# Layer 1's weight folds, its q swaps and the place of its folded projection in a two-layer encoder

## The chip, the cores and the metric

The kernel runs on one core of one Trainium2 chip. Every time is in device microseconds of that core; one launch does the whole computation. A profile is one execution taken by the hardware profiler.

## What is computed

Two layers over 272 tokens (16 learned tokens and 256 of the input) of width 2048, in float32. Cut to what matters here:

```
h = RMSNorm(x)
q, k, v, f, ga, gf = split(h @ W_in)                # 8 q heads, 2 kv heads of 128; f has 8 groups of 128 channels
q, k = rope_2d(RMSNorm(q)), rope_2d(RMSNorm(k))     # rotary: swaps neighbouring 32-channel quarters of a head
a = softmax(q k^T / sqrt(128)) v @ W_attn_br
s = Re(2-D DFT of f over positions and group channels) @ W_four
x = x + (sigmoid(ga) * a + sigmoid(gf) * s) @ W_out
x = x + (silu(dwconv3(RMSNorm(x) @ W_up_gate)) * (RMSNorm(x) @ W_up_val)) @ W_down
```

## The kernel before

Activations lie with channels on the 128 partitions and tokens along the row. Every float32 matrix product is made of three matmuls: each operand is split into a rounded high part and a rest (`wh` and `wl` for weights, `xHL` for activations), and high x high, high x rest and rest x high are summed.

**The weight stream.** All weights of both layers come in chunks of 512 KB ([128, 4, 256]), in one list `order` that is written out ahead (from L140). `load_raw` (L176 to L180) issues a chunk's load on SyncE (SP, line L179) into one of four `raw` buffers. `split_w` makes `wh` on ScalarE (ACT, L213) and `wl` on VectorE (DVE, L214); there are three buffers of each. `advance` keeps loads up to four chunks ahead of the splits and splits two ahead of the matmuls. `group` (from L242) runs one pair of output tiles: four chunks for an input of 2048 channels, 24 matmuls to a chunk (L270 to L272).

**Shadow work.** Smaller work (statistics, rotary, attention, Fourier steps) is written as generators that `push` puts into a list. `group` calls `step` after every second pair of products, 16 times in a group of four chunks; `step` lets one generator run to its next `yield n`, where n is the number of steps to wait. `until(hold, flag)` forces generators on until a flag is set. The instructions of each engine are then put in an order by the framework's scheduler, so a generator's place in the source is a wish, not the final place.

**The folds.** Layer 1's Fourier branch uses that a cosine is even and a sine odd: sums and differences of paired weight columns (and rows) do half the matmuls. They are made by `prefold` (L427 to L444) during the FFN of layer 0: 32 tiles of 512 KB, each loaded to `pfi` (L433), added and subtracted on VectorE into `pfo` (L439), and stored to `fw` in DRAM (L444). All transfers are issued on SP, among the weight loads. Layer 1 reads `fw` as part of its stream: 16 chunks for the folded projection f4, and two for each of eight `s` groups.

**The start of layer 1.** Groups k and v come first, then q group 0, then f4 (`folded_f`, from L661), then q groups 1, 2 and 3, then gates and branches. f4 uses all eight PSUM banks and runs 18 matmuls in each of its 16 chunks; it calls no `step`. `fold_pair` prepares its folded input on VectorE and ACT, four pairs ahead and four during f4. `folded_chan` then does the channel DFT.

**The q path.** `head_evac` takes a q group out of PSUM (L745 on ACT, L746 on VectorE). `q_stage` (from L848) makes the head sums, swaps the quarters with four DMAs of 68 KB (`swap`, L756 to L760, issued on ACT at L759), and after seven or eight steps does the rotary (`rope`, L762 to L767: L763, L764, L765 and L767 on VectorE, L766 on ACT). The same swap serves k. In layer 1 the q tiles `qH` and `qL` share their memory with f4's result `E` and with the v tile, so `q_stage` of group 0 waits until after the channel DFT of f4.

Of the kernel before, what the change touches and what calls it, by code (L numbers as in the profile page):

```python
# [16 lines left out]
P = 128  # L17
# [111 lines left out]
def encoder_kernel(ctx, tc, xT, params, consts, bmat, cfold, csign, w_fl, w_f64c, w_in, w_abr, w_four, w_f64, w_out, w_up, w_down, outT):  # L129
# [11 lines left out]
    for l in range(DEPTH):  # L141
        def g(w, mg, k0, k1):
            return [(w[l, mg, c], CW) for c in range(k0 // CW, k1 // CW)]
        if l == 0:
            f01 = [g(w_in, IN_F + i, 0, KT) for i in range(2)]
            order.append(((l, "f01"), [ch for pr in zip(*f01) for ch in pr]))
            for i in range(2, 4):
                order.append(((l, "f", i), g(w_in, IN_F + i, 0, KT)))
        order.append(((l, "k", 0), g(w_in, IN_K, 0, KT)))
        order.append(((l, "v", 0), g(w_in, IN_V, 0, KT)))  # L150
        for i in range(4):
            order.append(((l, "q", i), g(w_in, IN_Q + i, 0, KT)))
            if l == 1 and i == 0:
                order.append(((l, "f4"), [(fw[kt], CW) for kt in range(KT)]))
        for half in range(2):
            for kind, j in BRANCH_ORDER[half]:
                w, off, n = {"ga": (w_in, IN_GA, KT), "gf": (w_in, IN_GF, KT), "s": (w_four, 0, 8), "a": (w_abr, 0, 8)}[kind]
                chs = [(fw[KT + 2 * j + c], CW) for c in range(2)] if (l, kind) == (1, "s") else g(w, off + j, 0, n)
                order.append(((l, kind, j), chs))
            for mg in range(8):  # L160
                order.append(((l, "o", half, mg), g(w_out, mg, 8 * half, 8 * half + 8)))
        k0 = 0
        for c, n in enumerate(FF_SPLIT):
            for i in range(k0 // MG, (k0 + n) // MG):
# [55 lines left out]
    def push(gen, wait=0):  # L220
        shadow.append([wait, gen])
# [204 lines left out]

    def prefold(pool):  # L427
        src = [w_fl[k] for k in range(KT)] + [w_four[1, j, c] for j in range(NG) for c in range(2)]
        ins, outs = {}, {}
        for j in range(len(src) + 2):  # L430
            if j < len(src):
                ins[j] = pool.tile([P, CW, MG * P], F32, tag="pfi", name=f"pfi{j}", bufs=2)
                nc.sync.dma_start(ins[j], src[j])  # L433
            yield 2
            if 0 <= j - 1 < len(src):
                a, o = ins.pop(j - 1), pool.tile([P, CW, MG * P], F32, tag="pfo", name=f"pfo{j}", bufs=2)
                half = (lambda t_, q: t_[:, :, q * P:(q + 1) * P]) if j - 1 < KT else (lambda t_, q: t_[:, 2 * q:2 * q + 2])
                for q, op in ((0, ALU.add), (1, ALU.subtract)):
                    nc.vector.tensor_tensor(half(o, q), half(a, 0), half(a, 1), op=op)  # L439
                    yield 1  # L440
                outs[j - 1] = o
            yield 2
            if j >= 2:
                nc.sync.dma_start(fw[j - 2], outs.pop(j - 2))  # L444

    def norm_stats(holder):
        ps = psum.tile([P, 512], F32, tag="aux", name="ps_nst")
# [25 lines left out]
    for l in range(DEPTH):  # L473
# [4 lines left out]
        hold = {}  # L478

        with tc.tile_pool(name=f"mix{l}", bufs=1) as mp:  # L480
            E = mp.tile([P, 4, 2, TH] if last else [P, NG, T], F32, tag="q1", name="E")
            e64 = mp.tile([2 * NG, TH], F32, tag="u", name="e64", bufs=2) if last else None
            AHn = 3 * 4 * T
            ALn = 2 * 4 * T
# [176 lines left out]
            def folded_f(slots, E):  # L661
# [6 lines left out]
                for k in range(KT):  # L668
                    i = st["next"]
                    advance(i + 1 + LOOK)  # L670
                    pump(i)
                    h, lo_ = splits.pop(i)
                    st["next"] += 1
                    sl = slots[k % NS]
                    for g in (0, 1, 2, 3):
                        for e in range(2):
                            w = slice(e * P, (e + 1) * P)
                            o2 = ps[g][e][:, :2 * TH].rearrange("p (r n) -> p r n", r=2)
                            nc.tensor.matmul(o2, h[:, g, w], sl[:, e], start=k == 0, stop=False)
                            if g == e == 0:  # L680
                                for r in range(2):
                                    nc.tensor.matmul(p64, w64s[:, k, :], sl[:, 0, r, :], start=False, stop=False)
                            nc.tensor.matmul(ps[g][e][:, :TH], lo_[:, g, w], sl[:, e, 0, :], start=False, stop=k == KT - 1)
                        pump()
                        if k == KT - 1:
                            for e in range(2):
                                nc.scalar.copy(E[:, g, e, :], ps[g][e][:, TH:2 * TH])
                                nc.vector.tensor_tensor(E[:, g, e, :], ps[g][e][:, :TH], E[:, g, e, :], op=ALU.add)
                            if g == 0:
                                nc.scalar.copy(e64, p64)  # L690
                    if k % 2 and k + NS < KT:
                        fold_pair((k + NS - 1) // 2, slots)
# [63 lines left out]
            def swap(hp):  # L756
                qs = rt("qs")
                for b in range(4):
                    nc.scalar.dma_start(qs[32 * b:32 * b + 32, :, :], hp[32 * (b ^ 1):32 * (b ^ 1) + 32, :, :])  # L759
                return qs  # L760

            def rope(hp, qs, H, L):  # L762
# [51 lines left out]
                until(hold, "keys")  # L814
            else:
                drain()
            vt = mp.tile([P, NKV, 3 * P], F32, tag="q2", name="vt")
            for m in range(MG):
                nc.vector.tensor_tensor(vt[:, m, P:3 * P], ps[m][:, NM:T], rstdB[:, NM:T], op=ALU.mult)
                nc.vector.tensor_tensor(vt[:, m, 0:P].rearrange("p (a b) -> p a b", b=NM), _rep(ps[m][:, 0:NM], P // NM),  # L820
# [26 lines left out]

            def q_stage(i, qp, qsq):  # L848
                kv, j = i // 2, i % 2
                sl = slice(2 * i, 2 * i + 2)  # L850
# [18 lines left out]
                rope(qp, qs, qH[:, sl, :], qL[:, sl, :])  # L869
                if j:  # L870
                    rqs.append(rq)
                    if kv == 0:
# [10 lines left out]
            def attention(kv, rq):  # L883
                nc.vector.tensor_scalar(rq, rq, 1.0 / math.sqrt(HD), None, op0=ALU.mult)
                qm = mp.tile([P, 2, 2, 4, NM], F32R, tag="qm", name="qm")
                for j, src in enumerate((qH, qL)):
                    nc.scalar.copy(qm[:, j], src[:, 4 * kv:4 * kv + 4, 0:NM].bitcast(F32).unsqueeze(1).to_broadcast([P, 2, 4, NM]))
# [7 lines left out]
                def scores(item):  # L895
                    if item is None:
                        lh, ll, rcol = qmh, qml, rq[:, 8:9]
                    else:
                        h, i = item
                        c0, c1 = BLK[1 + i]  # L900
                        lh, ll = qH[:, 4 * kv + h, c0:c1], qL[:, 4 * kv + h, c0:c1]
# [44 lines left out]
                        nc.vector.tensor_tensor(x3, src[32:48, 2], x3.bitcast(F32), op=ALU.subtract)  # L946

                def values(h):
                    hg = 4 * kv + h
# [6 lines left out]
                    nc.scalar.copy(qH[:, hg, lo:T], po[:, :W])  # L956
                    nc.vector.tensor_tensor(qL[:, hg, lo:T], po[:, :W], qH[:, hg, lo:T].bitcast(F32), op=ALU.subtract)
# [20 lines left out]
                while ready:  # L978
                    values(ready.pop(0))
                    yield 1  # L980

            for i in range(4):
                ps = group((l, "q", i), xr(lo), W)
                qq = head_evac(ps, prm[:, P_QN + l:P_QN + l + 1], "qp", lo)
                if last and i == 0:
                    until(hold, "vt")
                    until(hold, "ahead")
                    folded_f(slots, E)
                    o1_tiles()
                    push(folded_chan(E), 1)  # L990
                    q0 = qq
                    continue
                if i == int(last):
                    until(hold, "vt")
                    until(hold, "fold")
                    qH = mp.tile([P, NH, T], F32R, tag="q1", name="qH")
                    qL = mp.tile([P, NH, T], F32R, tag="q2", name="qL")
                    if last:
                        push(q_stage(0, *q0), 1)
                push(q_stage(i, *qq), 4)  # L1000


            def gate(kind, i):
# [11 lines left out]
            for half in range(2):  # L1015
                mH = mL = None
                for kind, i in BRANCH_ORDER[half]:
# [19 lines left out]
                    else:  # L1037
                        if mH is None:
# [5 lines left out]
                        ps = group((l, "a", i), lambda kt: (qH[:, kt, lo:T], qL[:, kt, lo:T]), W)  # L1044
# [140 lines left out]
```

## Time and profile before

| | |
|---|---|
| median of 3 runs | 2612.56 us (2611.66 to 2616.31) |
| the profiled execution's own time | 2610.09 us |
| its span, first to last instruction | 2608.3 us |
| granted TensorE clock, mean | 0.997 |
| PE busy | 2578.4 us, 99% |
| VectorE, ACT busy | 1719.6 us, 1215.6 us |
| moved by DMA | 499.19 MB, mean 191 GB/s |

The stages lie in the span as follows: layer 0's input and mixing up to about 533 us, its FFN to 1355, layer 1's k, v, q and f4 to 1482, its gates, branches and output to 1856, its FFN to the end. A page of the profile gives busy time by engine; its groups and the other views name an instruction by line, engine and the tiles that it writes and reads (`wl<-raw,wh`). "Idle before" is the time for which the engine stood in front of an instruction, and the arrow names what came last of what it waited for. SPq is SyncE's queue, which issues DMAs; PE is TensorE's matmul and PEld its weight load, which overlap, so that a busy PE is not one at full speed. A table by stages gives for each stretch the length, then busy time and count by engine, the clock, the DMA engines' share and GB/s.

### The profile page before, as it was taken

To read this page: it belongs to the slowest core of one execution; us is meant where nothing else is said; L and a number is where in the kernel's file an instruction comes from. 1 tells how busy PE (TensorE), PEld (TensorE's weight loads), DVE (VectorE), ACT (ScalarE), POOL (GpSimd) and SP (SyncE) were. 2 spreads that over 40 slices of the span, in tenths; PEclk is the share of its full clock that TensorE was granted. 3 is DMA by queue.
4 is the path that set the end of the run, shared out by engine and by line. 5 is a ranking of instruction groups with operands and counts; after the bars stand their busy time and mean duration, and the time that the engine had idled before them with its cause. 6 is when DMAs were issued, how large, how long until landed. Compare 5 with 4: busy or idle time off the path is not lost. (4 is left out here: it accounts for less than half of the span.)

```text
span 2608.3 us, 47795 instructions
## 1 busy us (share of the span) xinstructions
PE 2578.4 (99%) x19604; PEld 2507.6 (96%) x19604; DVE 1719.6 (66%) x2742; ACT 1215.6 (47%) x1762; POOL 20.5 (1%) x40
## 2 busy tenths in 40 slices
PE   9999999999899999999999999999999999999999
PEld 8999999999899999999999999999999998899988
DVE  7687767777666445656568777666766665566654
ACT  5455434543344334444445455445555543344543
POOL 0000000000000000000000000000000000000000
PEclk9999999999999999999999999999999999999999
DMA  6545655589865555555556446656555556555564
GB/s 232 167 147 162 194 183 187 181 283 331 300 232 178 172 177 176 173 178 173 175 178 205 142 143 196 192 191 193 186 185 186 185 187 187 186 186 186 186 198 158
DMA packets 142810, 499.19 MB, mean 191 GB/s; under 512 B 16368, under 2 KB 23152, under 8 KB 142592
## 3 DMA queue, kind: packets, MB, share of 16 engines
q1 hardware_dynamic: 136944, 491.23, 58.2%
q10 hardware_dynamic: 5648, 4.92, 0.6%
q8 instruction: 153, 2.51, 0.4%
q14 instruction: 65, 0.53, 0.1%
HBM read 474.43 MB, written 18.87 MB: 189 GB/s over the span
## 5 line engine op out<-in xcount | busy, mean ns | idle before, releaser
L214 DVE TENSOR_TENSOR wl<-raw,wh 128x1024 fp32r<-128x1024 f32 (+1 forms) x850 | 1036.2, 1221 | 717.5 <-ACT wh L213 712.8
L213 ACT CAST wh<-raw 128x1024 fp32r<-128x1024 f32 (+1 forms) x850 | 887.8, 1047 | 1013.9 <-issue 152.8
L272 PE MATMUL ps_ug<-xHL,wl 128*128 128x272 f32 (+1 forms) x1408 | 401.5, 286 | 2.6 <-DVE wl L214 2.5
L270 PE MATMUL ps_ug<-xHL,wh 128*128 128x272 f32 (+1 forms) x1408 | 402.2, 286 | 1.9 <-ACT wh L213 1.9
L271 PE MATMUL ps_ug<-xHL,wh 128*128 128x272 f32 (+1 forms) x1408 | 402.1, 286 | 0.0
L270 PEld LDWEIGHTS ps_ug<-xHL,wh 128*128 128x128 f32 x1408 | 265.4, 189 | 3.8 <-ACT wh L213 2.8
L272 PEld LDWEIGHTS ps_ug<-xHL,wl 128*128 128x128 f32 x1408 | 264.4, 188 | 4.1 <-DVE wl L214 3.9
L271 PEld LDWEIGHTS ps_ug<-xHL,wh 128*128 128x128 f32 x1408 | 265.5, 189 | 0.1
L266 PE MATMUL ps_uv<-xHL,wh 128*128 128x512 f32 x704 | 247.7, 395 | 0.0
L266 PE MATMUL ps_d<-gHL,wh 128*128 128x512 f32 x664 | 233.1, 395 | 0.0
L271 PE MATMUL ps_d<-gHL,wh 128*128 128x272 f32 (+1 forms) x744 | 214.4, 288 | 0.0
L270 PE MATMUL ps_d<-gHL,wh 128*128 128x272 f32 (+1 forms) x744 | 214.1, 288 | 0.0
L272 PE MATMUL ps_d<-gHL,wl 128*128 128x272 f32 (+1 forms) x744 | 214.0, 288 | 0.0
L270 PE MATMUL ps_uv<-xHL,wh 128*128 128x272 f32 x704 | 204.9, 291 | 8.1 <-ACT wh L213 8.1
L272 PE MATMUL ps_uv<-xHL,wl 128*128 128x272 f32 x704 | 203.9, 292 | 2.7 <-DVE wl L214 2.7
L271 PE MATMUL ps_uv<-xHL,wh 128*128 128x272 f32 x704 | 204.6, 291 | 0.0
L267 PE MATMUL ps_uv<-xHL,wl 128*128 128x256 f32 x704 | 197.7, 281 | 0.0
L267 PE MATMUL ps_d<-gHL,wl 128*128 128x256 f32 x664 | 186.6, 281 | 0.0
L266 PEld LDWEIGHTS ps_uv<-xHL,wh 128*128 128x128 f32 x704 | 132.4, 188 | 29.9
L266 PEld LDWEIGHTS ps_d<-gHL,wh 128*128 128x128 f32 x664 | 125.0, 188 | 29.2
L270 PE MATMUL ps_ga<-xHL,wh 128*128 128x272 f32 (+1 forms) x512 | 148.2, 289 | 0.0
L270 PE MATMUL ps_gf<-xHL,wh 128*128 128x272 f32 (+1 forms) x512 | 147.2, 287 | 0.0
(322 smaller groups left out, 5854.0 us busy)
## 6 DMA issues: line engine op xcount, KB each, us to landing
raw<-in_w_up SPq DMA_DIRECT2D x352, 512.0 KB, 3.5
raw<-in_w_in SPq DMA_DIRECT2D x191, 512.0 KB, 3.6
raw<-in_w_down SPq DMA_DIRECT2D x176, 512.0 KB, 3.5
raw<-in_w_out SPq DMA_DIRECT2D x64, 512.0 KB, 3.6
raw<-in_w_abr SPq DMA_DIRECT2D x32, 512.0 KB, 3.6
fw<-pfo SPq DMA_DIRECT2D x32, 512.0 KB, 7.7
raw<-fw SPq DMA_DIRECT2D x32, 512.0 KB, 4.2
raw<-in_w_four SPq DMA_DIRECT2D x16, 512.0 KB, 3.8
```

What stands on the lines that cost most here:

```text
L213: nc.scalar.copy(h[:, a:b], r[:, a:b])
L214: nc.vector.tensor_tensor(lo[:, a:b], r[:, a:b], h[:, a:b].bitcast(F32), op=ALU.subtract)
L266: nc.tensor.matmul(o2, h[:, c, sl], ab, start=kt == 0, stop=False)
L267: nc.tensor.matmul(o, lo[:, c, sl], ab[:, 0, :], start=False, stop=kt == nk - 1)
L270: nc.tensor.matmul(o, h[:, c, sl], a, start=kt == 0, stop=False)
L271: nc.tensor.matmul(o, h[:, c, sl], b, start=False, stop=False)
L272: nc.tensor.matmul(o, lo[:, c, sl], a, start=False, stop=kt == nk - 1)
```

## The change

Four edits, all in the code above.

- `prefold` has one loop step less. It loads tile j and in the same place issues the store of tile j - 1; then waits 12 steps, adds, waits 3, subtracts, waits 3, and waits 12 more. Before, the waits were 2, 1, 1 and 2, the add was for the tile loaded one turn earlier, and the store came at the end of the turn after that.
- `swap` issues its four DMAs on SP.
- In layer 1 the folded projection comes after q group 1, in `order` and in the loop; q_stage of groups 0 and 1 is pushed when the group is done. To make that possible `E` and the v tile of layer 1 have buffers of their own (`q1b`, `q2b`), and the q tiles are two of four heads each instead of one of eight.
- In the last chunk of `folded_f` the output groups run in the order 2, 3, 0, 1.

```diff
-            if l == 1 and i == 0:
+            if l == 1 and i == 1:
                 order.append(((l, "f4"), [(fw[kt], CW) for kt in range(KT)]))
...
-        for j in range(len(src) + 2):
+        outs = {}
+        for j in range(len(src) + 1):
             if j < len(src):
-                ins[j] = pool.tile([P, CW, MG * P], F32, tag="pfi", name=f"pfi{j}", bufs=2)
-                nc.sync.dma_start(ins[j], src[j])
-            yield 2
-            if 0 <= j - 1 < len(src):
-                a, o = ins.pop(j - 1), pool.tile([P, CW, MG * P], F32, tag="pfo", name=f"pfo{j}", bufs=2)
+                a = pool.tile([P, CW, MG * P], F32, tag="pfi", name=f"pfi{j}", bufs=2)
+                nc.sync.dma_start(a, src[j])
+            if j:
+                nc.sync.dma_start(fw[j - 1], outs.pop(j - 1))
+            yield 12
+            if j < len(src):
+                o = pool.tile([P, CW, MG * P], F32, tag="pfo", name=f"pfo{j}", bufs=2)
...
                 for q, op in ((0, ALU.add), (1, ALU.subtract)):
                     nc.vector.tensor_tensor(half(o, q), half(a, 0), half(a, 1), op=op)
-                    yield 1
-                outs[j - 1] = o
-            yield 2
-            if j >= 2:
-                nc.sync.dma_start(fw[j - 2], outs.pop(j - 2))
+                    yield 3
+                outs[j] = o
+            yield 12
...
-                    for g in (0, 1, 2, 3):
+                    for g in ((2, 3, 0, 1) if k == KT - 1 else (0, 1, 2, 3)):
...
                 for b in range(4):
-                    nc.scalar.dma_start(qs[32 * b:32 * b + 32, :, :], hp[32 * (b ^ 1):32 * (b ^ 1) + 32, :, :])
+                    nc.sync.dma_start(qs[32 * b:32 * b + 32, :, :], hp[32 * (b ^ 1):32 * (b ^ 1) + 32, :, :])
...
+            qH, qL = [], []
             for i in range(4):
                 ps = group((l, "q", i), xr(lo), W)
                 qq = head_evac(ps, prm[:, P_QN + l:P_QN + l + 1], "qp", lo)
-                if last and i == 0:
-                    until(hold, "vt")
-                    until(hold, "ahead")
...
+                if last:
+                    if i in (0, 2):
+                        until(hold, "vt" if i == 0 else "fold")
+                        for t_, n in ((qH, "q1"), (qL, "q2")):
+                            t_.append(mp.tile([P, 4, T], F32R, tag=n + "ab"[i // 2], name=n))
...
+                push(q_stage(i, *qq), 4)
+                if last and i == 1:
                     until(hold, "ahead")
                     folded_f(slots, E)
                     o1_tiles()
                     push(folded_chan(E), 1)
```

More of the change, by code (lines that the diff above doesn't have):

```diff
@@ L428, in prefold @@
         src = [w_fl[k] for k in range(KT)] + [w_four[1, j, c] for j in range(NG) for c in range(2)]
-        ins, outs = {}, {}
-        for j in range(len(src) + 2):
+        outs = {}
+        for j in range(len(src) + 1):
             if j < len(src):
-                ins[j] = pool.tile([P, CW, MG * P], F32, tag="pfi", name=f"pfi{j}", bufs=2)
-                nc.sync.dma_start(ins[j], src[j])
-            yield 2
-            if 0 <= j - 1 < len(src):
-                a, o = ins.pop(j - 1), pool.tile([P, CW, MG * P], F32, tag="pfo", name=f"pfo{j}", bufs=2)
-                half = (lambda t_, q: t_[:, :, q * P:(q + 1) * P]) if j - 1 < KT else (lambda t_, q: t_[:, 2 * q:2 * q + 2])
+                a = pool.tile([P, CW, MG * P], F32, tag="pfi", name=f"pfi{j}", bufs=2)
[5 more added lines that the diff above has]
+                o = pool.tile([P, CW, MG * P], F32, tag="pfo", name=f"pfo{j}", bufs=2)
+                half = (lambda t_, q: t_[:, :, q * P:(q + 1) * P]) if j < KT else (lambda t_, q: t_[:, 2 * q:2 * q + 2])
                 for q, op in ((0, ALU.add), (1, ALU.subtract)):
                     nc.vector.tensor_tensor(half(o, q), half(a, 0), half(a, 1), op=op)
-                    yield 1
-                outs[j - 1] = o
-            yield 2
-            if j >= 2:
-                nc.sync.dma_start(fw[j - 2], outs.pop(j - 2))
+                    yield 3
+                outs[j] = o
+            yield 12
     def norm_stats(holder):
@@ L480, in encoder_kernel @@
         with tc.tile_pool(name=f"mix{l}", bufs=1) as mp:
-            E = mp.tile([P, 4, 2, TH] if last else [P, NG, T], F32, tag="q1", name="E")
+            E = mp.tile([P, 4, 2, TH] if last else [P, NG, T], F32, tag="q1b" if last else "q1", name="E")
             e64 = mp.tile([2 * NG, TH], F32, tag="u", name="e64", bufs=2) if last else None
@@ L816, in encoder_kernel @@
                 drain()
-            vt = mp.tile([P, NKV, 3 * P], F32, tag="q2", name="vt")
+            vt = mp.tile([P, NKV, 3 * P], F32, tag="q2b" if last else "q2", name="vt")
             for m in range(MG):
@@ L849, in q_stage @@
                 kv, j = i // 2, i % 2
-                sl = slice(2 * i, 2 * i + 2)
+                sl = slice(2 * j, 2 * j + 2)
                 if j == 0:
@@ L868, in q_stage @@
                 yield 8 - j
-                rope(qp, qs, qH[:, sl, :], qL[:, sl, :])
+                rope(qp, qs, qH[kv][:, sl, :], qL[kv][:, sl, :])
                 if j:
@@ L886, in attention @@
                 for j, src in enumerate((qH, qL)):
-                    nc.scalar.copy(qm[:, j], src[:, 4 * kv:4 * kv + 4, 0:NM].bitcast(F32).unsqueeze(1).to_broadcast([P, 2, 4, NM]))
+                    nc.scalar.copy(qm[:, j], src[kv][:, :, 0:NM].bitcast(F32).unsqueeze(1).to_broadcast([P, 2, 4, NM]))
                 qmh, qml = (qm[:, j].rearrange("p r h t -> p (r h t)") for j in range(2))
@@ L900, in scores @@
                         c0, c1 = BLK[1 + i]
-                        lh, ll = qH[:, 4 * kv + h, c0:c1], qL[:, 4 * kv + h, c0:c1]
+                        lh, ll = qH[kv][:, h, c0:c1], qL[kv][:, h, c0:c1]
                         rcol = rq[:, 2 * h + i:2 * h + i + 1]
@@ L948, in values @@
                 def values(h):
-                    hg = 4 * kv + h
                     po = psum.tile([P, 512], F32, tag="aux", name="ps_pv")
@@ L955, in values @@
                     nc.tensor.matmul(po[:, :W], V3[:, kv, :], PH[:, 2, h, lo:T], start=False, stop=True)
-                    nc.scalar.copy(qH[:, hg, lo:T], po[:, :W])
-                    nc.vector.tensor_tensor(qL[:, hg, lo:T], po[:, :W], qH[:, hg, lo:T].bitcast(F32), op=ALU.subtract)
+                    nc.scalar.copy(qH[kv][:, h, lo:T], po[:, :W])
+                    nc.vector.tensor_tensor(qL[kv][:, h, lo:T], po[:, :W], qH[kv][:, h, lo:T].bitcast(F32), op=ALU.subtract)
                 items = [None] + [(h, i) for h in range(4) for i in range(2)]
@@ L984, in encoder_kernel @@
                 qq = head_evac(ps, prm[:, P_QN + l:P_QN + l + 1], "qp", lo)
-                if last and i == 0:
-                    until(hold, "vt")
+                if last:
[3 more added lines that the diff above has]
+                            t_.append(mp.tile([P, 4, T], F32R, tag=n + "ab"[i // 2], name=n))
+                elif i == 0:
+                    until(hold, "vt")
+                    until(hold, "fold")
+                    for t_, n in ((qH, "q1"), (qL, "q2")):
+                        t = mp.tile([P, NH, T], F32R, tag=n, name=n)
+                        t_ += [t[:, 0:4], t[:, 4:8]]
+                push(q_stage(i, *qq), 4)
+                if last and i == 1:
                     until(hold, "ahead")
@@ L990, in encoder_kernel @@
                     push(folded_chan(E), 1)
-                    q0 = qq
-                    continue
-                if i == int(last):
-                    until(hold, "vt")
[L995 to L1000, printed above, removed]
             def gate(kind, i):
@@ L1043, in encoder_kernel @@
                             mL = mLf[:, :8 * T].rearrange("p (k t) -> p k t", k=8)
-                        ps = group((l, "a", i), lambda kt: (qH[:, kt, lo:T], qL[:, kt, lo:T]), W)
+                        ps = group((l, "a", i), lambda kt: (qH[kt // 4][:, kt % 4, lo:T], qL[kt // 4][:, kt % 4, lo:T]), W)
                         for m in range(MG):
```

## Prediction

> **What bounds the kernel now.** I read the page first, then the table by stages, then the waits of the worst stage, then the transfers. The page:
>
> ```profile
> span 2608.3 us, 47795 instructions
> PE 2578.4 (99%) x19604; PEld 2507.6 (96%) x19604; DVE 1719.6 (66%) x2742; ACT 1215.6 (47%) x1762; POOL 20.5 (1%) x40
> DMA  6545655589865555555556446656555556555564
> ```
>
> TensorE is busy for 99% of the span, so only places where it waits or runs slowly can give anything. The DMA row shows one bump, slices 8 to 10. The table by stages covers it, with an undisturbed stretch below for scale:
>
> ```profile
> 533.00:620.00 87.00, 86.66 (x689) 86.36 (x688) 67.26 (x106) 38.23 (x51) 1.22 (x1) 1.00 0.94 320
> 620.00:727.00 107.00, 91.77 (x662) 87.59 (x661) 71.37 (x107) 38.46 (x50) 0.00 (x0) 0.95 0.90 315
> 740.00:1234.00 494.00, 494.00 (x3936) 494.00 (x3936) 276.44 (x356) 208.34 (x252) 0.00 (x0) 1.00 0.54 175
> ...
> 1394.00:1432.00 38.00, 35.16 (x293) 33.57 (x290) 31.55 (x47) 23.21 (x41) 0.24 (x2) 1.00 0.78 242
> 1432.00:1464.00 32.00, 32.00 (x260) 30.97 (x259) 22.38 (x56) 14.18 (x34) 2.16 (x5) 1.00 0.45 133
> 1464.00:1482.00 18.00, 16.00 (x116) 15.34 (x115) 13.52 (x29) 9.01 (x18) 0.00 (x0) 0.91 0.51 148
> ```
>
> The columns after the length are busy time and count of PE, weight load, DVE, ACT, POOL, then clock, DMA share, GB/s. The long stretch gives the pace: 494.00 / 3936 = 0.1255 us per matmul, so one weight chunk (24 matmuls, one 512 KB load) takes 3.01 us. At that pace 689 matmuls take 86.5 us and 662 take 83.1: the first layer's FFN loses 0.5 + 23.9 = **24.4 us** from 533 to 727. The third row from layer 1 loses 18.00 - 116 x (32.00 / 260) = **3.7 us**, and the folded projection before it (1394 to 1432) has 38.00 - 35.16 = **2.8 us** idle. Those are the three places the change can pay in.
>
> Who is late in the first of them (waits from 533 to 730, then SP's own, then the transfers from 533 to 727):
>
> ```profile
> ACT wh L213 <- DMA raw<-in_w_up: 50.2, 22, 5.0
> PE ps_uv L270 <- ACT wh L213: 8.1, 3, 2.9
> ```
> ```profile
> SPq L433 <- DVE pfo L439: 57.9, 17, 7.0
> ```
> ```profile
> DMA packets 16877, 61.59 MB, mean 317 GB/s; under 512 B 1878, under 2 KB 1878, under 8 KB 16862
> raw<-in_w_up SPq DMA_DIRECT2D x55, 512.0 KB, 6.3
> fw<-pfo SPq DMA_DIRECT2D x32, 512.0 KB, 7.7
> pfi<-in_w_fl SPq DMA_DIRECT2D x16, 512.0 KB, 6.1
> pfi<-in_w_four SPq DMA_DIRECT2D x16, 512.0 KB, 5.2
> ```
>
> The weight split (ACT, L213) waits 50.2 us for loads. The folds of layer 1's weights add 32 loads and 32 stores of the same 512 KB to 55 weight loads, and together they get 317 GB/s at a DMA share of 0.90 to 0.94, against 175 GB/s when the weights go alone. This stretch is bound by the supply of weights, and nothing else in the kernel loses so much.
>
> **The change part by part.**
>
> 1. *The folds.* The fold's four waits in steps sum to 30 instead of 6 per tile, and a group has 16 steps, so the source reads as if a tile came every 7.5 chunks. The built order does not follow that: as the scheduler arranged SP, the first fold load stands behind weight load 173 in both kernels, and the last fold store behind load 226 before and 243 after. The folds are spread over 70 chunks where they had 53, not over 240. So, with 0.524 MB per transfer:
>  - before: (53 + 64) x 0.524 = 61.3 MB, at 317 GB/s 193.5 us; TensorE needs 53 x 3.01 = 159.5. The gap is 34.0, of which 24.4 was lost, so the four weight buffers ahead took up 9.6 (three chunks).
>  - after: (70 + 64) x 0.524 = 70.3 MB, 221.6 us; TensorE needs 70 x 3.01 = 210.8. The gap is 10.8, less the same 9.6: 1.2.
>
>  I take **2 us lost** where 24.4 were, a gain of 22.4. Bounds: nothing lost, a gain of 24.4; or the supply of the stretch's poorest third with no help from the buffers, 70.3 MB at 310 GB/s = 226.6, 15.8 lost, a gain of 8.6:
>
> ```profile
> 533.00:580.00 47.00, 46.66 (x371) 46.37 (x370) 37.58 (x63) 22.97 (x31) 1.22 (x1) 1.00 0.92 310
> ```
>
>  The store of a tile is now issued behind the load of the next, so SP meets results that are mostly done. The work itself is the same 64 halves (0.684 us each, below) on VectorE.
>
>  A part of the 24.4 is not waiting. The time line:
>
> ```profile
> 680.18 0.29 PE L272 MATMUL ps_ug<-xHL,wl 128*128 128x272 f32 x1
> 683.40 0.59 PE L270 MATMUL ps_uv<-xHL,wh 128*128 128x272 f32 x1 [2.94 <-ACT wh L213]
> ...
> 688.90 0.43 PE L271 MATMUL ps_uv<-xHL,wh 128*128 128x272 f32 x1
> ```
>
>  After 2.94 us of idling, matmuls take 0.43 us for 0.29 for over 5 us, and the mean clock of the stage is 0.95: 5% of 107 us, 5.4 us. Idling alone is 107.00 - 91.77 = 15.2. The rest lies in small late starts. [...]
>
> 2. *The swaps, from ACT to SP.* Each swap is four issues:
>
> ```profile
> qs<-qp ACTq DMA_DIRECT2D x32, 68.0 KB, 4.1
> r<-in_w_f SPq DMA_DIRECT2D x16, 64.0 KB, 4.3
> ```
> ```profile
> L759 ACTq DMA_DIRECT2D qs<-qp x4: 592/614/1597, 1468.8 to 1471.8; - x4
> L759 ACTq EVENT_SEMAPHORE  x1: 3792/3792/3792, 1465.0 to 1465.0; - x1
> ```
> ```profile
> 1475.21 0.72 DVE L763 TENSOR_TENSOR qs<-qs,cst 128x544 f32<-128x544 f32 x1 [2.08 <-DMA qs<-qp]
> ```
> ```profile
> 1477.82 0.39 PE L272 MATMUL ps_q<-xHL,wl 128*128 128x258 f32 x1 [1.71 <-DVE wl L214]
> ```
>
>  This is the 3.7 us at 1464: ACT stood 3.79 us at a swap for VectorE's q, the splits behind it waited, the swap left late, VectorE waited 2.08 for it, and TensorE 1.71 for the split after that. 40 issues x 0.61 = 24 us of ACT go; ACT is 47% busy, so they are worth nothing by themselves, but its standing still is. On SP the weight loads queue behind the swap: about 2.4 us of issue each time. They run four buffers ahead (4 x 3.01 = 12 us) and outside the folds land in 3.5, so the cover is over 6 us; without it ten swaps would cost 24. A transfer of this size from SP lands in 4.3 us against 4.1, so the swap is not much later.
>
> ```profile
> raw<-in_w_up SPq DMA_DIRECT2D x352, 512.0 KB, 3.5
> ```
>
>  In the built order most swaps leave SP two splits (6 us) ahead of VectorE's use. One does not: the third q group of layer 1, whose last quarter stands behind load 475, which needs split 471 finished, while L763 follows split 471 after two short steps. There VectorE waits again. I leave 1.1 us of the 3.7 and take a gain of **2.6** (bounds: all 3.7; or a second such loss, -3.7).
>
> 3. *The folded projection between groups 1 and 2, separate q tiles, the last chunk's order.* The instructions are the same ones (19435 rows on PE in both built orders). The rotary work and the head sums of groups 0 and 1 move before and into the projection, so VectorE has less in the group after it (attention starts in chunk 472 instead of 469) and more inside it, where a chunk has only 38 / 16 = 2.4 us. VectorE is 31.55 of 38 us busy there already. At the end, TensorE no longer has the channel matmul right behind the last chunk. I take **nothing**: bounds +2.8 (all idling goes) and -3.0 (four rotary steps of 0.72 us from the L763 row above come late for a chunk).
>
> Sum: 22.4 + 2.6 = 25.0. The profiled execution took 2610.09 us (span 2608.3), so it would be 2585.1; the median of the runs shown, 2612.56, lies 2.5 above it. Forecast: 2587.6, given as **2588**.
>
> **The rivals.**
>
> - *The supply stays short* (15.8 lost instead of 2): for it, 333 GB/s would be needed for full pace (70.3 MB in 210.8 us), more than the mean of 317; against it, the loss before came only once the buffers were empty. 2612.6 - 8.6 - 2.6 = 2601. At 287 GB/s the folds would lose as much as before, that is, the spreading would do nothing: 2610.
> - *The swaps stay late on SP.* [...] Price: two losses of 3.7 us in layer 1 where there was one. 2612.6 - 22.4 + 3.7 = 2594. Against it stands the 4.3 us of the SP row.
> - *Slower: VectorE stands at the folds.* Its row:
>
> ```profile
> L439 DVE TENSOR_TENSOR pfo<-pfi x64: 681/684/694, 539.0 to 724.7; 128x512 f32<-128x512 f32 x64
> ```
> ```profile
> DMA to landing us min/median/max: 3.5/5.9/7.9
> ```
>
>  In the built order after, each fold stands two splits (6.0 us) behind the point where its load can leave; before it was up to six. A landing beyond 6.0 blocks VectorE and the split behind. VectorE is 67.26 / 87 = 77% busy, so of the 6.6 us per tile it can give up 1.5. From a typical landing of 7.5 us on, each further us costs 32; above 8.3 us the 25.0 us of gains are gone, and at 8.5 the time is 2620. Against it: the median is 5.9, the longest 7.9.
>
> **How the numbers follow.** Forecast (2580 to 2594) 0.66; short supply (2595 to 2605) 0.14; late swaps (2592 to 2600) 0.08; spreading without effect (about 2610) 0.06; VectorE at the folds 0.06. Range 2580 to 2603: the low end has every loss gone (24.4 + 3.7 + 2.8), the high end leaves out the last two cases. A measurement of this kernel can tell some 0.2% (5.2 us) from no change. Faster than that 0.88, within it 0.06, slower 0.06.
>
> **What would show it.** Folds: from 533 to about 750, TensorE's idling near 2 us, the clock at 1.00, 315 to 335 GB/s, fold stores ending about 20 us later. If ACT's wait for weights stays above 20 us there, the supply was short; if VectorE waits for fold loads by more than 1.5 us a tile, the third rival holds. Swaps: no long ACT wait at L759, the clock at 1.00 in the q groups of layer 1; a VectorE wait for a swap followed by a TensorE wait for a split speaks for the second rival. Projection: TensorE's idling between 0 and 6 us. I am wrong if new waits appear in layer 0's q groups, where I count nothing.

## The result, and the profile after

The changed kernel takes **2591.70 us** (2590.24 to 2592.22, 5 runs) where the kernel before took 2614.45 (2611.66 to 2618.74, 5 runs beside it): a ratio of 0.9911, 95% interval [0.9897, 0.9926], 22.8 us less. The forecast was 2588 in a range of 2580 to 2603. The profiled executions took 2590.24 and 2610.09, a gain of 19.9; the stages below are theirs.

The page after, by the same rows as before:

```profile
span 2588.5 us, 47816 instructions
...
PE 2570.9 (99%) x19604; PEld 2503.6 (97%) x19604; DVE 1720.3 (66%) x2742; ACT 1215.5 (47%) x1762; POOL 19.5 (1%) x40
...
DMA  7545555589985555555556446566555555555564
```

The bump in the DMA row starts in the same slice, 8, and lasts one slice longer. The table by stages says what became of it; the third row is the folded projection, which now starts at 1384:

```profile
533.00:620.00 87.00, 87.00 (x693) 86.84 (x692) 67.93 (x106) 40.39 (x53) 1.22 (x1) 1.00 0.91 319
620.00:727.00 107.00, 106.38 (x837) 105.09 (x836) 79.73 (x120) 46.93 (x63) 0.00 (x0) 1.00 0.93 326
...
1384.00:1426.00 42.00, 36.77 (x288) 35.39 (x286) 29.86 (x41) 22.59 (x38) 0.24 (x2) 0.92 0.60 204
```

From 620 to 727 TensorE now does 837 matmuls where it did 662, at a clock of 1.00, and idles for 0.62 us. But the projection takes 42.2 us for the work that took 36.5 before, at a clock of 0.92. From the start times of the matmuls in the two traces: the FFN of layer 0, up to layer 1's first key matmul, went from 821.3 to 798.9 us (**-22.4**), and layer 1's mixing, from there to its first FFN matmul, from 501.5 to 503.6 (**+2.1**). So one place gave all the gain and another took a little back.

In the FFN of layer 0 SyncE no longer stands at fold loads. Before, it stood there for 57.9 us (L433), until the adds of L439 had freed one of the two `pfi` buffers, and hardly at fold stores:

```profile
SPq L444 <- DVE pfo L439: 4.8, 2, 2.7
```

Now the loads cost it 0.5 us and the stores (L435, behind the adds, now L441) 8.7, and VectorE stands at the landing of fold loads instead. SP's waits, then VectorE's, 533 to 730:

```profile
SPq L179 <- DVE wl L214: 94.7, 46, 5.5
...
SPq L435 <- DVE pfo L441: 8.7, 7, 2.6
...
SPq L433 <- PE ps_o L272: 0.5, 1, 0.5
```
```profile
DVE pfo L441 <- DMA pfi<-in_w_four: 21.3, 12, 3.8
DVE pfo L441 <- DMA pfi<-in_w_fl: 13.9, 10, 2.7
```

L179, a weight load, waits long, but this is no loss: SyncE is far enough ahead to wait for a free weight buffer. ACT's wait for a weight load, 50.2 us before, no longer appears among the longest.

In the projection, VectorE's time line, then TensorE's, then the DMAs that SP issued:

```profile
1404.70 0.50 DVE L652 SCALAR_TENSOR_TENSOR hB<-hf,prm,hB 128x276 fp32r<-128x276 f32 x1
1409.75 0.73 DVE L763 TENSOR_TENSOR qs<-qs,cst 128x544 f32<-128x544 f32 x1 [4.55 <-DMA qs<-qp]
1410.39 0.72 DVE L764 TENSOR_TENSOR qp<-qp,cst 128x544 f32<-128x544 f32 x1
1411.03 1.22 DVE L214 TENSOR_TENSOR wl<-raw,wh 128x1024 fp32r<-128x1024 f32 x1
```
```profile
1412.30 0.33 PE L683 MATMUL ps_f<-hA,wl 128*128 128x138 f32 x1 [3.27 <-DVE wl L214]
```
```profile
1401.19 1.89 SPq L759 DMA_DIRECT2D qs<-qp  x3
1403.18 0.53 SPq L179 DMA_DIRECT2D raw<-fw  x1
1403.75 0.59 SPq L759 DMA_DIRECT2D qs<-qp  x1
```

Read it from the bottom: the swap of q group 1 leaves SP from 1401.2 to 1404.3. VectorE is at that group's first rotary step (L763) at 1405.2, stands there for 4.55 us, and only then makes the next rest of a weight (L214). TensorE waits 3.27 us for that rest, and the clock is at half from 1413.7 to 1420.5. This is a loss of the kind that the second rival described, at a place that I had not named.

### The profile page after: what moved, and what is told of

The parts are those of the page before. It is cut to its first block, busy times and chain, and to the rows that moved or that the text cites. A ratio compares the mean times of both kernels' runs of the same rounds, so it can differ in the third digit from the quotient of the medians.

```text
span 2588.5 us, 47816 instructions
## 1 busy us (share of the span) xinstructions
PE 2570.9 (99%) x19604; PEld 2503.6 (97%) x19604; DVE 1720.3 (66%) x2742; ACT 1215.5 (47%) x1762; POOL 19.5 (1%) x40
## 4 chain that ended last, share of the span: by engine, by line
PE 92%; DVE 3%; DMA 3%; ACT 1%; issue 1%; SPq 0%; POOL 0%; DVEq 0%; ACTq 0%
PE ps_uv L266 6%; PE ps_ug L271 6%; PE ps_ug L272 6%; PE ps_ug L270 6%; PE ps_d L266 6%; PE ps_d L270 4%; PE ps_d L271 4%; PE ps_d L272 4%; PE ps_uv L267 3%; PE ps_d L267 3%; PE ps_uv L272 3%; PE ps_uv L270 3%; PE ps_uv L271 3%; PE ps_gf L270 2%; PE ps_gf L271 2%; PE ps_o L271 2%
## 5 line engine op out<-in xcount | busy, mean ns | idle before, releaser
L214 DVE TENSOR_TENSOR wl<-raw,wh 128x1024 fp32r<-128x1024 f32 (+1 forms) x850 | 1036.1, 1222 | 676.7 <-ACT wh L213 671.0
```

Of the source, the lines that this page charges most:

```text
L214: nc.vector.tensor_tensor(lo[:, a:b], r[:, a:b], h[:, a:b].bitcast(F32), op=ALU.subtract)
```

## The experiments

All times are medians, each ratio against the kernel before measured beside it (the row of before is the first of these; the others gave 2614.14 to 2616.46). e5 and e6 have two runs each, the others four or more. The last three columns are stages of the profiled execution, from the matmuls' start times: FFN of layer 0, folded projection from first to last matmul, mixing of layer 1. Edit 1 is the new fold loop, 2 the swaps on SP, 3 the place of the projection with its tiles and last chunk.

| run | edits | us | ratio, 95% interval | FFN 0 | projection | mixing |
|---|---|---|---|---|---|---|
| before | none | 2614.45 | 1 | 821.3 | 36.5 | 501.5 |
| after | 1, 2, 3 | 2591.70 | 0.9911 [0.9897, 0.9926] | 798.9 | 42.2 | 503.6 |
| e1 | 1 | 2588.94 | 0.9900 [0.9882, 0.9918] | 802.6 | 38.5 | 503.0 |
| e11 | 2 | 2610.62 | 0.9982 [0.9972, 0.9992] | 823.1 | 35.0 | 498.5 |
| e12 | 1, 2 | 2584.70 | 0.9889 [0.9875, 0.9902] | 799.2 | 34.9 | 497.2 |
| e2 | 2, 3 | 2616.13 | 1.0007 [0.9998, 1.0016] | 823.3 | 41.5 | 502.5 |
| e4 | 1, 3 | 2589.05 | 0.9907 [0.9892, 0.9922] | 797.4 | 41.1 | 503.2 |
| e3 | 1, 2, 3, sine step late | 2589.36 | 0.9907 [0.9892, 0.9922] | 800.4 | 37.2 | 498.9 |
| e5 | fold transfers alone | 2597.23 | 0.9935 [0.9915, 0.9955] | 805.9 | 36.4 | 501.7 |
| e6 | fold adds alone | 2583.70 | 0.9883 [0.9863, 0.9903] | 796.3 | 36.8 | 501.3 |
| e7 | 1 paced, 2, 3 | 2587.75 | 0.9898 [0.9881, 0.9914] | 796.3 | 40.9 | 502.4 |
| e8 | e7 and e3 | 2585.66 | 0.9891 [0.9876, 0.9906] | 796.3 | 40.7 | 502.1 |
| e10 | e8, cosine step late too | 2580.77 | 0.9872 [0.9859, 0.9886] | 796.3 | 34.9 | 496.0 |
| e13 | 1 paced, 2 | 2582.97 | 0.9878 [0.9861, 0.9894] | 796.3 | 34.9 | 496.8 |

### e1: the folds alone

The kernel before with the fold loop of the diff, and nothing else of it.

> The kernel before with the new fold loop alone. Theory (the folds' supply was the whole gain, the other edits together cost about 2 us in layer 1): the FFN of layer 0 loses about 2.5 us instead of 24.4, layer 1's start is as before, so about 22 us less than before, 2592 or a little lower, and not slower than the full change. Rival (the gain needs the other edits too): a gain of 18 us or less.

25.7 us of gain: the whole of the change's gain comes from this edit (the 2.9 us more than the change's 22.8 lie within the intervals). Its stage table:

```profile
533.00:620.00 87.00, 87.00 (x691) 86.56 (x690) 66.36 (x104) 39.72 (x52) 1.22 (x1) 1.00 0.90 315
620.00:727.00 107.00, 103.44 (x808) 102.83 (x807) 78.23 (x117) 45.68 (x61) 0.00 (x0) 0.98 0.93 321
```

In this profiled execution (2593.69 us, the slowest of its four) 3.56 us of idling were left from 620 to 727, where the changed kernel had 0.62. The same schedule thus loses between 1.1 us (e4) and 6.3 us (e1) of the floor of 796.3: it stands at the edge of what it needs.

### e2: everything but the folds

The changed kernel with the fold loop of before.

> The changed kernel with the old fold loop. Theory: the 24 us in layer 0's FFN are lost again and layer 1 pays about 2 us on top: 2614 to 2619 beside 2614.5 before. Rival (swaps on SP and the later folded projection gain by themselves, as forecast, 2.6 us): 2610 to 2613.

No gain, and by the median 1.5 us more: edits 2 and 3 together are worth nothing, where the forecast gave them 2.6. The projection takes 41.5 us here too, so its loss has nothing to do with the folds.

### e3: the sine step of q group 1 behind the projection

```diff
-            def rope(hp, qs, H, L):
-                nc.vector.tensor_tensor(qs, qs, bc2(sin), op=ALU.mult)
+            def rope(hp, qs, H, L, late=False):
+                if late:
+                    one = small.tile([P, 1], F32, tag="mx", name="one")
+                    nc.vector.tensor_scalar(one, E[:, 1, 1, 0:1], 0.0, 1.0, op0=ALU.mult, op1=ALU.add)
+                    for m in range(MG):
+                        nc.vector.scalar_tensor_tensor(qs[:, m], qs[:, m], one, sin, op0=ALU.mult, op1=ALU.mult)
+                else:
+                    nc.vector.tensor_tensor(qs, qs, bc2(sin), op=ALU.mult)
...
-                rope(qp, qs, qH[kv][:, sl, :], qL[kv][:, sl, :])
+                rope(qp, qs, qH[kv][:, sl, :], qL[kv][:, sl, :], last and i == 1)
```

`late` is set for q group 1 of layer 1 alone. `E` is the projection's result, so the step can't be put ahead of its end.

> The changed kernel, with the first rotary step of q group 1 in layer 1 made to depend on the last result of the folded projection, so that VectorE cannot stand at that swap inside the projection; the swap stays where it is. Theory (the 4.5 us wait of VectorE at this swap makes TensorE's 3.3 us wait and the half clock after it): both go, about 6 us less than the changed kernel, 2585 to 2587. Rival (VectorE's load inside the projection is the cause, and the wait only stands in front of it): less than 2 us gained, 2590 to 2592.

The projection falls from 42.2 to 37.2 us and the mixing from 503.6 to 498.9: most of the stall was VectorE at L763. The total, 2589.36 us, falls between the two ranges expected, and 2.3 us below the changed kernel where 6 were forecast; the FFN of layer 0, 1.5 us longer in this execution, hides part of the gain. A new wait is left, at the next rotary step:

```profile
1411.92 0.73 DVE L770 TENSOR_TENSOR qp<-qp,cst 128x544 f32<-128x544 f32 x1 [2.32 <-DMA qs<-qp]
```

This step, the cosine step, writes `qp` in place, and the swap is a DMA that reads `qp`: it waits until the swap has read.

### e4: the swaps back on ACT

The changed kernel with `nc.scalar.dma_start` in `swap`.

> The changed kernel with the swaps issued on ACT again. Theory (SP's queue makes the swap of q group 1 late inside the projection): the swap leaves ACT earlier and VectorE's wait of 4.5 us is under 2 us, but ACT stands at the swaps of the later groups again, about 3.7 us lost there: 2588 to 2592. Rival (the issuing queue does not matter, only how close the rotary step stands): the projection keeps its loss of 7 us and the later loss comes back too, 2593 to 2596.

The projection still takes 41.1 us. Of the waits in it, two rows; then one line each of VectorE's, ACT's and TensorE's time line:

```profile
ACT wh L213 <- DVE hB L652: 2.3, 1, 2.3
...
DVE qs L763 <- DMA qs<-qp: 1.5, 1, 1.5
```
```profile
1409.81 0.72 DVE L763 TENSOR_TENSOR qs<-qs,cst 128x544 f32<-128x544 f32 x1 [1.49 <-DMA qs<-qp]
```
```profile
1411.96 0.64 ACT L766 CAST q<-qp 128x544 fp32r<-128x544 f32 x1 [3.95 <-DVE qp L765]
```
```profile
1413.11 0.34 PE L683 MATMUL ps_f<-hA,wl 128*128 128x138 f32 x1 [2.42 <-DVE wl L214]
```

VectorE waits less for the swap, 1.49 us, but only because it comes to it later, at 1408.3 instead of 1405.2: among other things its own split waited 1.9 us, while ACT stood 2.3 us at the swap. The swap's last quarter left ACT at 1404.9 and landed at 1409.7; from SP it left at 1403.8 and landed at 1409.6, so L763 starts at 1409.8 in both. Then ACT stands 3.95 us at its own part of the rotary (L766), with the next weight split behind it. The choice of the queue does not remove the loss; it comes with the rotary of group 1 standing among the projection's splits.

Each side of the expectation has a part: the time, 2589.05, and VectorE's wait are as the theory said, and the projection keeps its loss, as the rival said. The loss behind the later groups that both expected does not come back: from 1426 to 1530 us TensorE waits 1.1 us in all, though ACT stands 3.9 us at a swap there too.

### e5 and e6: the fold's transfers alone, its adds alone

Both have the fold spacing of before. e5 stores each loaded tile as it is, without the adds, from four buffers:

```diff
-                ins[j] = pool.tile([P, CW, MG * P], F32, tag="pfi", name=f"pfi{j}", bufs=2)
+                ins[j] = pool.tile([P, CW, MG * P], F32, tag="pfi", name=f"pfi{j}", bufs=4)
...
-                    nc.vector.tensor_tensor(half(o, q), half(a, 0), half(a, 1), op=op)
```

e6 makes the adds on a constant tile, without the loads and with two stores instead of 32; layer 1 reads the unfolded weights where they lie:

```diff
-                nc.sync.dma_start(ins[j], src[j])
+                ins[j] = fix
...
+                if j < 4:
+                    nc.sync.dma_start(fw[j - 2], outs.pop(j - 2))
```

> The kernel before with its old fold loop, but without the adds and subtractions: each tile is stored to DRAM as it was loaded (four buffers), so that layer 1's Fourier branch computes with unfolded weights. Theory (supply: 117 transfers of 512 KB in the time of 53 chunks): TensorE still loses 18 to 28 us in layer 0's FFN, with the DMA engines over 0.85 busy and 310 to 340 GB/s. Rival (SP and VectorE wait for each other through the adds, and the supply would do): under 8 us lost.

> The kernel before with its old fold loop, with the 64 adds and subtractions on a constant tile, but without the fold loads and all but two of the fold stores; layer 1's Fourier branch computes with unfolded weights. Theory (supply): under 2 us lost in layer 0's FFN, 175 to 190 GB/s there, 2588 to 2594. Rival (VectorE's work of 64 x 0.684 us is what crowds the stage): 10 us or more lost.

e5, then e6, by stages:

```profile
533.00:620.00 87.00, 87.00 (x694) 86.92 (x694) 53.91 (x81) 42.02 (x56) 0.85 (x1) 1.00 0.96 342
620.00:727.00 107.00, 100.66 (x778) 97.94 (x777) 58.83 (x82) 43.96 (x57) 0.00 (x0) 1.00 0.93 336
```
```profile
533.00:620.00 87.00, 87.00 (x694) 86.92 (x693) 86.13 (x140) 41.35 (x55) 2.31 (x2) 1.00 0.55 183
620.00:727.00 107.00, 107.00 (x854) 107.00 (x854) 67.45 (x95) 48.69 (x64) 0.00 (x0) 1.00 0.53 177
```

The adds alone lose nothing, as the theory of e6 said, though VectorE is 99% busy in the first row (the total, 2583.70, is even 4 us below the expected range). The transfers alone lose 805.9 - 796.3 = 9.6 us of the 25.0 that before lost, which lies between the theory of e5 (18 to 28) and its rival (under 8), and they run at 336 to 342 GB/s. So 317 GB/s was not the ceiling of the supply, and neither part makes the whole loss alone. What only before has is the chain of the two: SP stood 57.9 us at fold loads until the adds had freed a buffer, with weight loads behind them. That this chain costs the other 15 us is not shown, for SP stands at fold loads in e5 too, there until a store has read one of the four buffers (SP's waits, 533 to 730):

```profile
SPq L433 <- DMA fw<-pfi: 69.2, 22, 5.5
```

e5 has four load buffers instead of two as well, so how the 15 us divide between adds and buffers is open.

### e7: each fold load tied to the progress of the FFN

```diff
                 a = pool.tile([P, CW, MG * P], F32, tag="pfi", name=f"pfi{j}", bufs=2)
+                if "t" in tick:
+                    nc.vector.tensor_copy(a[:, 0, 0:1], tick["t"])
                 nc.sync.dma_start(a, src[j])
```

`tick["t"]` is a column of the FFN's last result so far. The scheduler can't draw the load ahead of it, and the folds spread over 236 weight loads instead of 70.

> The changed kernel with one copied element more per tile: each fold load depends on a result of the running FFN, so that the scheduler cannot move it ahead; the 32 tiles then lie over 236 weight loads instead of 70. Theory (supply): at 0.66 MB per chunk, 220 GB/s, nothing is lost, so the 1 to 4 us that the FFN still loses go: 1 to 4 us below the changed kernel, 2588 to 2590. Rival (what is left there comes from VectorE standing at fold loads, 41 us in all): the same gain, but with VectorE still waiting for fold loads by more than 10 us.

The FFN of layer 0 is at its floor, 796.3 us, and TensorE has no idling at 220 to 226 GB/s:

```profile
533.00:620.00 87.00, 87.00 (x693) 86.92 (x693) 59.28 (x90) 40.09 (x53) 0.85 (x1) 1.00 0.65 220
620.00:727.00 107.00, 107.00 (x855) 107.00 (x854) 71.12 (x106) 49.54 (x64) 0.00 (x0) 1.00 0.65 226
```

All four kernels with this edit (e7, e8, e10, e13) show 796.3. VectorE waits 1.3 us in all for fold loads, where the changed kernel waited 40.6, so the rival of e7 is out. The time, 2587.75, is 4.0 us below the changed kernel's, at the edge of what was expected.

### e8 and e10: paced folds, and the rotary of group 1 behind the projection

e8 is e7 with e3's edit. e10 has the cosine step late as well:

```diff
                     for m in range(MG):
                         nc.vector.scalar_tensor_tensor(qs[:, m], qs[:, m], one, sin, op0=ALU.mult, op1=ALU.mult)
+                        nc.vector.scalar_tensor_tensor(hp[:, m], hp[:, m], one, cos, op0=ALU.mult, op1=ALU.mult)
```

> Both: the paced folds, and the first rotary step of q group 1 in layer 1 behind the folded projection. Theory (the two losses are in different stages and add up): 2591.7 less 1 to 4 less 4 to 5, 2583 to 2587. Rival (what one stage gives comes back as a loss elsewhere): 2588 or more.

e8 was a miss: its median, 2585.66, lies in the theory's range, but the projection still takes 40.7 us where 4 to 5 us were to go. VectorE stands at the cosine step now, and longer than in e3:

```profile
1408.45 0.72 DVE L774 TENSOR_TENSOR qp<-qp,cst 128x544 f32<-128x544 f32 x1 [3.83 <-DMA qs<-qp]
```

Removing one reader of the swap only uncovers the writer behind it.

> As the run before (folds paced, sine step of q group 1 behind the folded projection), and now the cosine step, which writes qp in place while the swap still reads it, is put behind the projection as well. Theory (the projection loses its 6 us because VectorE stands, in order, at one of the two rotary steps of q group 1: at the sine step until the swap has landed, at the cosine step until the swap has read): with neither step ahead of the projection's weight splits no VectorE wait over 1 us is left inside the projection, its half-clock stretch goes, the part from the keys to the first gate block takes 119 to 122 us where it took 125.8, and the time is 2580 to 2583 us. Rival (the projection is late for another reason, its own evacuations or the short chunks, and the stall moves to the next instruction): 125 us for that part and 2584.5 to 2587 us. Second rival (the late rotary steps make the scores of group 1 late): the gain inside the projection is given back in the group after it, 2584 to 2588 us.

With both steps out of the way the wait, the half clock and 6 us are gone, and nothing comes back later: from the keys to the first gate block it takes 120.0 us where 119 to 122 were forecast, and the mixing 496.0:

```profile
1382.00:1417.00 35.00, 33.46 (x288) 32.64 (x285) 27.53 (x38) 22.18 (x37) 0.25 (x2) 1.00 0.75 246
```

The same 288 matmuls, at a clock of 1.00, in 35 us for 42. By its median this is the fastest kernel of the study, 34 us below the one before.

### e11 and e12: the swaps alone; folds and swaps without the third edit

> The kernel before with the swaps on SyncE's queue and nothing else. Forecast's step (the swap on SyncE lands before VectorE wants it): the 3.7 us lost behind the third group's swap are gone, 2611 to 2612.5 us in a call whose kernel before takes 2614.5. Rival (the swap is late on either queue because the rotary step stands too close behind it): the wait stays, 2613.5 to 2616 us.

> The new fold schedule and the swaps on SyncE, with the folded projection back behind the first q group and the two projections' tiles and last chunk as before, so this is the changed kernel without its third part. If the third part costs what the changed kernel lost in layer 1 (the projection now stands over the rotary step of group 1): 2586 to 2588.5 us, layer 1's mixing 499.5 to 501.5 us instead of 503.6. If the place of the projection means nothing and there is a wait of that size wherever it stands: 2589 to 2592 us, mixing 502.5 to 504 us.

e11 by stages, its projection and the two stretches that the prediction showed behind it:

```profile
1397.00:1432.00 35.00, 33.86 (x287) 32.69 (x285) 28.66 (x40) 21.47 (x33) 0.24 (x2) 1.00 0.71 238
1432.00:1464.00 32.00, 31.35 (x248) 29.91 (x249) 22.98 (x62) 13.89 (x36) 2.16 (x5) 1.00 0.44 145
1464.00:1482.00 18.00, 17.68 (x148) 17.46 (x147) 13.28 (x29) 10.77 (x20) 0.00 (x0) 1.00 0.48 139
```

The kernel before did 116 matmuls in the last of these, at a clock of 0.91; here it is 148 at 1.00. The swaps alone gain 4.2 us by the medians, a little more than the first case of the expectation, and 3.0 in the mixing of the profiled execution. What goes is TensorE's wait: VectorE still stands 2.11 us at a swap there.

```profile
1478.52 0.73 DVE L763 TENSOR_TENSOR qs<-qs,cst 128x544 f32<-128x544 f32 x1 [2.11 <-DMA qs<-qp]
```

e12 adds the folds: 30.2 us of gain, against 22.8 of the whole change, and its mixing is 2.3 us shorter than even the first case of its expectation said. So **the third edit costs the rest**: the mixing goes from 497.2 (e12) to 503.6 us (after), +6.4, with paced folds from 496.8 (e13) to 502.4 (e7), +5.6, and without the folds from 498.5 (e11) to 502.5 (e2), +4.0. The projection of e12:

```profile
1372.50:1407.50 35.00, 34.06 (x289) 32.88 (x286) 28.65 (x39) 21.67 (x33) 0.25 (x2) 1.00 0.70 238
```

### e13: e12 with paced folds

> The new fold schedule with each fold load tied to a result of the feed-forward blocks (so spread over all of layer 0's FFN), the swaps on SyncE, and no third part. If the two gains are of separate places and add up: layer 0's FFN 796.3 us as in the paced run, layer 1's mixing 497 us as in the run without the third part, and 2581 to 2582.5 us, the same as the best run so far without any edit to the rotary steps. If the projection behind the first q group costs something that the late rotary steps of the best run don't: 2583 to 2585 us, no better than unpaced.

Both gains are there by stage, 796.3 and 496.8, as the first case said; the median, 2582.97, lies just between the two ranges. Its ratio is the same as e10's within the intervals, with nothing done to the rotary: the simplest of the good kernels.

## Why the prediction was right, and where it was wrong

**The folds: right in size, half right in reason.** Forecast: 24.4 us of loss become 2, a gain of 22.4. Measured: 25.0 become 2.6 over the whole FFN (the floor is 796.3), a gain of 22.4. The built order was the right thing to read: fold adds end at 750 instead of 725 us, and the stage needed what 70 chunks need. But I took 317 GB/s for the most that the supply gives, and without the adds e5 got 339. The working held since at 70 chunks the stage needs little more than the old rate (70.3 MB in 210.8 + 9.6 us, 319 GB/s), and it got 319 to 326. That forecast and result agree to 0.1 us is luck: the same schedule took 797.4 to 802.6 us in the executions of e1, e3, e4, e12 and after.

The new loop does two things at once: it spreads the folds over 70 chunks, and it lets VectorE stand at fold loads where SP stood before. No run has one without the other. My estimate, from the prediction's working: at e5's 339 GB/s, 53 chunks need 61.3 MB / 339 GB/s = 180.8 us of supply, 21.3 more than TensorE's 159.5; less the 9.6 that the four weight buffers took up, 11.7 us would still be lost, and e5 did lose 9.6. So a better rate alone would not have done it. Spreading further does: at 236 chunks (e7) nothing is lost.

**The third rival was there and was absorbed**, as its own price said. The transfers from 533 to 727 after:

```profile
DMA packets 17174, 62.72 MB, mean 323 GB/s; under 512 B 1905, under 2 KB 1905, under 8 KB 17157
...
fw<-pfo SPq DMA_DIRECT2D x28, 512.0 KB, 6.4
pfi<-in_w_fl SPq DMA_DIRECT2D x16, 512.0 KB, 6.4
pfi<-in_w_four SPq DMA_DIRECT2D x14, 512.0 KB, 7.4
```

Fold loads land in 6.4 and 7.4 us, beyond the 6.0 that the built order leaves. VectorE stands at them for 21.3 + 13.9 = 35.2 us up to 730, some 1.2 per tile for the 30 loads of these rows, within the 1.5 that the prediction let it give up.

**The swaps: right alone, 2.6 forecast and 3.0 in the trace (e11).** That ACT's standing at a swap (3.79 us before) costs TensorE time behind the third group (1.71 us before), and that the swap on SP takes most of this away, is borne out, and so is that VectorE waits again at that group (2.11 us in e11). It is not general: in e4 ACT stands 3.9 us at a later swap, and TensorE waits 1.1 us in all from 1426 to 1530. Nor does the sentence "most swaps leave SP two splits (6 us) ahead" hold everywhere. Two splits are 6 us where a chunk takes 3.01; in the projection it takes 35 / 16 = 2.2, so there two splits are 4.4 us.

**The projection: the step that failed.** I gave edit 3 nothing, with -3.0 as the worst bound: four rotary steps of 0.72 us that come late. It cost 4.0 to 6.4 with the swaps on SP. (With the swaps on ACT it cost less: the mixing of e4 takes 503.2, that of the kernels without edit 2 and 3 takes 501.3 to 503.0, the last of these, e1, with a half-clock stretch of its own in the projection. The projection grows there as well, but the loss behind the third group's swap, which edit 2 takes away otherwise, goes too.) The bound counted the work that moves into the projection, and not what the moved steps wait for. They bring the swap's landing (L763) and its reading (L764) with them, into the one stretch where splits are needed every 2.2 us; VectorE stood 4.55 us, TensorE 3.27, and half clock for 6.8 us took 3.4 more. e10 shows that it is these two steps and nothing else of the edit: with them behind the projection, the edit costs nothing (496.0 against 496.8 in e13).

**The second rival came nearer in price, and e4 speaks against its cause.** It forecast a loss of 3.7 us more in layer 1, and put it down to swaps that stay late on SP; e4 shows the projection's loss (41.1 us, after 42.2) with the swaps on ACT, landing at the same moment (1409.7 us, after 1409.6). So the layer 1 part came out at +2.1 for -2.6 forecast, and that is nearly all of the difference between forecast and result: 25.0 us of gain forecast, 19.9 between the profiled executions.

## What to carry to other kernels

Here a step of 0.73 us that moved took a wait of 4.55 us with it: price the longest wait that a step may bring, by the pace of the stretch into which it moves, and not only its own busy time. The rate measured in the stretch that waited, 317 GB/s, was not a ceiling (339 in e5); run the transfers alone before you reason from one. Where a scheduler decides the order, a spacing in the source is a wish (the folds lay over 70 weight loads); a data dependence on the work that it should follow held (236 in e7).

## What the runs showed of the hardware

In these traces the half clock does not go by the length of one wait. These waits of TensorE come from e1 (1379 and 1463 us), then e3, then after:

```profile
1379.71 0.60 PE L679 MATMUL ps_f<-hA,wh 128*128 128x276 f32 x1 [0.78 <-DVE qp L746]
...
1462.97 0.39 PE L272 MATMUL ps_q<-xHL,wl 128*128 128x258 f32 x1 [2.79 <-DVE wl L214]
```
```profile
1390.55 0.39 PE L679 MATMUL ps_f<-hA,wh 128*128 128x276 f32 x1 [1.53 <-DVE qp L746]
```
```profile
1387.68 0.39 PE L679 MATMUL ps_f<-hA,wh 128*128 128x276 f32 x1 [1.53 <-DVE qp L746]
```

During the 0.78 us of e1, the third short wait in 3 us (0.64 and 0.24 us before it), the clock went to half, from 1379.3 to 1386.2; behind its 2.79 it stayed at 1.00, up to 1480. The same wait of 1.53 us at the same instruction was followed by 3.4 us of half clock in e3 (1391.2 to 1394.6), and by none in the changed kernel (clock 1.00 from 1376 to 1400).

In the kernel before the clock was at half from 659.1 to 662.5, from 683.0 to 689.8 and from 1478.3 to 1481.7 us, in the changed kernel from 1413.7 to 1420.5: with those of e1 and e3, each lasted some 3.4 or 6.8 us. No run varied TensorE's idle time by itself, so what sets the half clock off, and what decides how long it lasts, is open.
